# Which engine adds up the adaLN products for layer 3 while ConvFFN 2 runs

## The chip, the cores and the metric

One core of one Trainium2 chip runs the whole network as one program. The metric is the device time of one execution in microseconds; three executions of the kernel before took 1762.29, 1764.65 and 1765.87 us (median 1764.65). The tensor engine (PE) multiplies, the vector engine (DVE) and the scalar engine (ACT) work on tiles, GpSimd (POOL) works on tiles too and issues some transfers, and SyncE (SP) issues the weight transfers. Each engine executes its own queue strictly in order.

## The reference, cut to what matters

Four layers, each a token mixer followed by a gated convolutional feed-forward block (ConvFFN). Every sub-layer is modulated by six vectors per layer (adaLN) that come from one product of a condition vector with a large matrix:

```python
cond_lat = jax.nn.silu(c)
for i in range(DEPTH):
    mod_lat = (cond_lat @ ada_w[i] + ada_b[i])[:, None, :]      # 1024 x 6144 per layer
    sh1, sc1, g1, sh2, sc2, g2 = jnp.split(mod_lat, 6, axis=-1)
    ...
    h_lat = h_lat + g1 * y_lat
    v_lat = _modulate(_rmsnorm(h_lat, norm2_g[i]), sh2, sc2)
    h_lat = h_lat + g2 * _conv_ffn(v_lat, ...)

def _conv_ffn(u, w_up, conv_w, conv_b, w_down):
    hid = u @ w_up                                   # 1024 -> 5632
    hid = <depthwise convolution over 3 tokens>(hid) + conv_b
    val, gate = jnp.split(hid, 2, axis=-1)
    return (jax.nn.silu(gate) * val) @ w_down        # 2816 -> 1024
```

In layers 2 and 3 the blocks of interest work on the 256 latent tokens alone, and layer 3 needs its adaLN vectors for one condition only.

## The kernel before, in words

**ConvFFN.** `ffn` (L758) keeps PE supplied. Activations and weights are split into a high and a low part, and each product is three matmuls (`mm3`). The up-projection runs in 22 "pairs" f (one value tile, one gate tile, 48 matmuls of 256 columns), the down-projection in four parts of 8 output tiles d. Pairs and downs alternate: pairs 0 to 7, down of part 0, six pairs, down of part 1, and so on. Each pair writes two of four PSUM buffers `p`, so pair f+2 can start only when DVE has read pair f.

**What DVE does for each pair**, in the order of its queue for one condition: `al` (L819, low part of an earlier pair's activation, which the down-projection reads), a product `t` (L810), four convolution taps `t<-p` (L55; the last to read the pair's PSUM), and two subtractions `wlo` (L159) that make the low part of a weight block whose high part `whi` ACT has made. The end of `wlo` also frees the raw weight tile, so that SP can fetch the next block.

**The adaLN sums.** The product with `ada_w` is not done by PE directly. `ada_vec` (L297) is a generator with one step per loaded weight tile (`ada`, 1 MB, two buffers). It multiplies each tile by the condition values per partition and adds it to a running sum `ads`; at the end PE adds the sum over the partitions (`adp`) and turns it into columns (`adt`, `ada_turn`). `ffn` spreads the steps over its slots: `ada_slot` is called once after each pair and after every second d of the first three downs. Which engine adds is a letter per chunk: with "V" it is one operation on DVE, with "P" ACT multiplies in place and POOL adds:

```python
if i == 0:
    self.act(y, w[:, k], AF.Copy, scale=x)
elif eng == "V" or eng == "M" and i < 2:
    self.stt(y, w[:, k], x, y, ALU.mult, ALU.add)
else:
    ...
    self.act(t, w[:, k], AF.Copy, scale=x)
    self.nc.gpsimd.tensor_add(y, y, t)
```

The chunks of ConvFFN 2 are (layer 3, columns from 4, 4 wide), 8 tiles with one operation of 128x2048 each, and (layer 3, from 8, 2 wide), 4 tiles with two operations of 128x1024 each. In both, the first tile is written by ACT. Their tiles are fetched from POOL's queue (`ada_load`, L249), when the buffer before is free. The code puts a step behind the two `wlo` of its pair and ahead of the next pair's `al`.

Of the kernel before, what the change touches and what calls it, by code (L numbers as in the profile page):

```python
# [16 lines left out]
P = 128  # L17
# [27 lines left out]
class Net:  # L45
# [1929 lines left out]
    def run(self):  # L1975
        tc, nc, a = self.tc, self.nc, self.a
        with ExitStack() as es:
            pool = lambda n, **k: es.enter_context(tc.tile_pool(name=n, **k))
            self.cp = pool("cp", bufs=1)
            self.wp = pool("wp", bufs=1)  # L1980
            self.tp = pool("tp", bufs=1)
            self.up_ = pool("up_", bufs=1)
            PS = bass.MemoryType.PSUM
            self.psu = pool("psu", bufs=4, space=PS)
            self.psa = pool("psa", bufs=2, space=PS)
            self.psm = pool("psm", bufs=1, space=PS)
            es.enter_context(tc.manual_schedule())
            self.consts()
            blocks, glu0 = [], 0
            for l in range(DEPTH):  # L1990
                if l == 1:
                    glu0 = len(blocks)
                    blocks += [a["glu"][dp, kh] for dp, kh in GLU]
                if l == 2:
                    blocks += [a["qkv"][b] for b in (8, 9, 10, 11, 4, 0, 5, 1, 6, 2, 7, 3)] + [a["wo"][b] for b in range(4)]
                blocks += self.ffn_blocks(l)
            self.init_stream(blocks, 2, 2)
            self.limit = 0
            LC, LO = (0, 1), (0,)
            self.s5room = ExitStack()  # L2000
            self.sp = self.s5room.enter_context(tc.tile_pool(name="s5t", bufs=1, side="right"))
            with tc.tile_pool(name="s5p", bufs=1) as tp:
                self.start(tp, glu0)
            if self.stop == 4:
                return self.dump()

            tables = self.s5_tables()
            self.add_bg(tables)
            self.s5tab = {}
            self.ffn(0, LC, self.after_ffn(LC, self.s5_ahead), [(0, 10, 2), (1, 0, 4), (1, 4, 2)])  # L2010
            self.finish(tables)
            self.run_due(True)
            self.finish()
            if self.stop == 5:
                return self.dump()
            self.s5_mixer(1)
            self.finish()
            if self.stop == 10:
                return self.dump()
            self.ffn(1, LC, self.after_ffn(LC), [(1, 10, 2, "VV"), (2, 0, 4, "VV"), (2, 4, 4, "V"),  # L2020
                                                   (2, 8, 4, "P"), (3, 0, 4, "V")])
            self.finish()
            if self.stop == 11:
                return self.dump()
            self.nat_mixer(2)
            pm = self.pool_load(3)

            def pool_in(d):
                if d == 0:
                    self.pool_w(3, pm)  # L2030
                    self.pool_win(pm)
                    self.ada_init([(3, 10, 2, "M")], 1, (self.up_, self.u_bufs, 0, 2))
                    self.ada_ahead()

            self.ffn(2, LO, self.after_ffn(LO, pool_in), [(3, 4, 4, "P"), (3, 8, 2, "P")])
            r = self.rstd()
            us = self.pool_u(3, LO, r)
            self.sq_pe_start(LO)
            self._prep()
            self.pool_bias(3, 1, LO, pm)  # L2040
            for gp in range(2):
                self.pool_z(LO, pm, us, gp)
                next(self.ada_gen)
            self.pool_y(LO, pm, range(KD))
            self.ada_steps = [2, 6, 0, 0]
            self.r = self.rstd()
            self.ffn(3, LO, self.after_ffn(LO), None)
            self.final()
# [120 lines left out]
```

## Time and profile before

| what | value |
|---|---|
| median of three executions | 1764.65 us |
| the profiled execution | 1761.2 us, its span 1759.4 us |
| PE busy in the span | 1648.6 us (94%) |
| DVE busy | 1326.9 us (75%) |
| ACT busy | 804.5 us (46%) |
| POOL busy | 432.3 us (25%) |
| chain that ended last | PE 66%, DVE 13%, DMA 4%, ACT 4%, issue 4%, POOL 2% |

The span is what the trace covers; the execution's own time is 1.8 us longer. The busy shares are averages over all stages. ConvFFN 2 runs from about 1311 to 1532 us of the span, ConvFFN 3, of the same shape, from about 1560 to 1749 us. A timeline row gives start, duration, engine, line, operation, and in square brackets the idle time of the engine before it with what released it. A row of grouped instructions gives count, total busy time, mean duration in ns of one, and the idle time before them.

### The profile page before, as it was taken

How to read it: one execution, taken by the hardware profiler on the slowest of the kernel's cores; microseconds unless marked ns; L12 is line 12 of the kernel's file. 1: busy time of each engine (PE TensorE's matmuls, PEld its weight loads, DVE VectorE, ACT ScalarE, POOL GpSimd, SP SyncE). 2: the span in 40 equal slices, each digit the busy share in tenths (PEclk: the TensorE clock that was granted, in tenths of full speed). 3: DMA queues.
4: the chain of work that ended last, by engine and by line, in shares of the span. 5: the costliest groups of instructions: out<-in, count | busy, mean ns of one | idle time of the engine just before them, and what ended most of it. 6: DMA issues, size and time to landing. Idle time of an engine off the chain costs nothing.

```text
span 1759.4 us, 26668 instructions
## 1 busy us (share of the span) xinstructions
PE 1648.6 (94%) x10482; PEld 1364.8 (78%) x10482; DVE 1326.9 (75%) x1994; ACT 804.5 (46%) x1249; POOL 432.3 (25%) x330
## 2 busy tenths in 40 slices
PE   8889999998978899899999989999998799999998
PEld 4467777777768787687877867777688799889997
DVE  6768878899759667787877787546658889679776
ACT  4533323223253322643342634447657556475554
POOL 0015456574529301000000521102213404101001
PEclk9999999999998799999999999999999999999999
DMA  9658898787769644343548474333246666645553
GB/s 381 268 198 251 276 315 252 204 232 209 237 236 366 275 158 167 141 152 141 189 144 311 161 255 134 115 105 108 82 150 234 227 204 197 223 160 176 185 184 112
DMA packets 98182, 356.88 MB, mean 203 GB/s; under 512 B 14297, under 2 KB 37369, under 8 KB 72201
## 3 DMA queue, kind: packets, MB, share of 16 engines
q1 hardware_dynamic: 93400, 334.09, 56.2%
q0 software_dynamic: 4080, 18.99, 3.0%
q8 instruction: 83, 1.36, 0.3%
q10 hardware_dynamic: 576, 2.10, 0.3%
q14 instruction: 43, 0.34, 0.1%
HBM read 324.19 MB, written 30.94 MB: 202 GB/s over the span
## 4 chain that ended last, share of the span: by engine, by line
PE 66%; DVE 13%; DMA 4%; ACT 4%; issue 4%; POOL 2%; SPq 1%; DVEq 0%; ACTq 0%; POOLq 0%
PE p L61 33%; PE dn L61 15%; DVE wlo L159 5%; PE glu L61 4%; PE v L61 3%; PE k L61 2%; DVE t L55 2%; DMA s5fl<-s5dA 2%; PE wo L61 1%; PE q L61 1%; PE z L61 1%; PE adp L61 1%; ACT whi L58 1%; DVE al L819 1%; DMA raw<-in_wup_dram 1%
## 5 line engine op out<-in xcount | busy, mean ns | idle before, releaser
L61 PE MATMUL p<-uh,whi 128*128 128x512 f32 (+1 forms) x1408 | 485.5, 345 | 25.7 <-DVE t L55 15.3
L159 DVE TENSOR_TENSOR wlo<-raw,whi 128x1024 fp32r<-128x1024 f32 x334 | 401.2, 1243 | 123.3 <-ACT whi L58 122.1
L61 PE MATMUL p<-uh,wlo 128*128 128x512 f32 (+1 forms) x1408 | 480.0, 341 | 4.3 <-DVE wlo L159 2.5
L61 PE MATMUL p<-ul,whi 128*128 128x512 f32 (+1 forms) x1408 | 480.9, 342 | 0.1
L58 ACT ACTIVATE whi<-raw 128x1024 fp32r<-128x1024 f32 x352 | 318.3, 952 | 259.8 <-PE dn L61 83.4
L61 PEld LDWEIGHTS p<-uh,whi 128*128 128x128 f32 x1408 | 271.4, 193 | 68.9 <-issue 14.8
L61 PEld LDWEIGHTS p<-uh,wlo 128*128 128x128 f32 x1408 | 271.0, 192 | 35.8 <-DVE wlo L159 3.5
L61 PEld LDWEIGHTS p<-ul,whi 128*128 128x128 f32 x1408 | 271.3, 193 | 31.2 <-DVE ul L55 2.3
L61 PE MATMUL dn<-ah,wlo 128*128 128x512 f32 (+1 forms) x704 | 239.6, 340 | 8.5 <-DVE wlo L159 8.5
L61 PE MATMUL dn<-ah,whi 128*128 128x512 f32 (+1 forms) x704 | 240.9, 342 | 6.9 <-DVE h L55 4.1
L61 PE MATMUL dn<-al,whi 128*128 128x512 f32 (+1 forms) x704 | 239.0, 340 | 5.1 <-DVE al L819 5.1
L55 DVE SCALAR_TENSOR_TENSOR t<-p,conv_sb,t 128x510 f32<-128x510 f32 (+1 forms) x352 | 208.1, 612 | 27.3 <-ACT t L58 21.0
L321 POOL TENSOR_TENSOR ads<-ads,ada 128x2048 f32<-128x2048 f32 (+1 forms) x24 | 95.0, 3967 | 402.2 <-ACT ada L58 391.5
L61 PEld LDWEIGHTS dn<-ah,whi 128*128 128x128 f32 x704 | 134.9, 192 | 30.6 <-issue 10.2
L61 PEld LDWEIGHTS dn<-ah,wlo 128*128 128x128 f32 x704 | 134.8, 192 | 25.4 <-DVE wlo L159 10.9
L61 PEld LDWEIGHTS dn<-al,whi 128*128 128x128 f32 x704 | 134.6, 191 | 19.7 <-DVE al L819 5.6
L58 ACT ACTIVATE t<-p,conv_sb 128x512 f32<-128x512 f32 (+1 forms) x176 | 107.5, 660 | 49.5 <-PE p L61 49.4
L55 DVE SCALAR_TENSOR_TENSOR ads<-ada,cT_sb,ads 128x2048 f32<-128x2048 f32 (+1 forms) x56 | 116.7, 2116 | 8.1 <-DMA ada<-in_ada_dram 5.5
L55 DVE SCALAR_TENSOR_TENSOR h<-dn,mods,h 128x256 f32<-128x256 f32 x192 | 83.7, 476 | 40.8 <-PE dn L61 40.8
L58 ACT ACTIVATE ah<-t 128x512 fp32r<-128x512 f32 (+1 forms) x88 | 45.9, 523 | 148.9 <-DVE t L810 139.0
L58 ACT ACTIVATE t<-t 128x512 f32<-128x512 f32 (+1 forms) x88 | 45.9, 521 | 145.4 <-DVE t L55 137.7
L1316 POOL TENSOR_TENSOR s5ct<-s5bc,s5pw 128x512 f32<-128x512 f32 x32 | 44.1, 1377 | 219.5 <-DMA s5bc<-in_s5c_dram 144.5
(256 smaller groups left out, 2337.1 us busy)
## 6 DMA issues: line engine op xcount, KB each, us to landing
raw<-in_wup_dram SPq DMA_DIRECT2D x88, 1024.0 KB, 5.2
ada<-in_ada_dram SPq DMA_DIRECT2D x84, 1024.0 KB, 7.7
raw<-in_wdn_dram SPq DMA_DIRECT2D x32, 768.0 KB, 4.5
raw<-in_wdn_dram SPq DMA_DIRECT2D x32, 640.0 KB, 4.0
raw<-in_qkv_dram SPq DMA_DIRECT2D x12, 1024.0 KB, 5.0
ada<-in_ada_dram POOLq DMA_DIRECT2D x12, 1024.0 KB, 5.4
s5bt<-in_s5bT_dram SPq DMA_DIRECT2D x32, 256.0 KB, 7.4
s5fl<-s5dA SPq DMA_DIRECT2D x32, 256.0 KB, 7.1
```

The lines of the kernel that those rows point to most:

```text
L55: return self.nc.vector.scalar_tensor_tensor(out, in0, scalar, in1, op0=op0, op1=op1, **kw)
L58: return self.nc.scalar.activation(out, in_, func, **kw)
L61: return self.nc.tensor.matmul(out, lhsT, rhs, start=start, stop=stop)
L159: self.nc.vector.tensor_sub(lo[:, s], t[:, s], hi[:, s].bitcast(F32))
L321: self.nc.gpsimd.tensor_add(y, y, t)
L819: V.tensor_sub(lo[:, :n], tv, hi[:, :n].bitcast(F32))
L1316: G.tensor_tensor(ct[:, o], *x, op=ALU.mult)
```

## The change

In the chunks that ConvFFN 2 carries for layer 3, the letter "P" becomes "V":

```diff
-            self.ffn(2, LO, self.after_ffn(LO, pool_in), [(3, 4, 4, "P"), (3, 8, 2, "P")])
+            self.ffn(2, LO, self.after_ffn(LO, pool_in), [(3, 4, 4, "V"), (3, 8, 2, "V")])
```

So 7 + 6 multiplications on ACT and 7 + 6 additions on POOL are replaced by 7 + 6 `scalar_tensor_tensor` operations on DVE. The first tile of each chunk, the slots, the buffers and the queue of the `ada` transfers stay as they are.

DVE's queue around pairs 2 and 3 of ConvFFN 2, before (`p_...` are the PSUM tiles of a pair, `ads_4_0` the running sum of the first chunk, `ada_4_n` its tile n):

```order
L159 TENSOR_TENSOR wlo_10820<-raw_10681,whi_10817 128x1024 x2
L819 TENSOR_TENSOR al_10880<-t,ah_10879 128x256
L810 TENSOR_TENSOR t<-t 128x256
L55 SCALAR_TENSOR_TENSOR t<-p_10758,conv_sb,t 128x255 x2
L55 SCALAR_TENSOR_TENSOR t<-p_10759,conv_sb,t 128x255 x2
L159 TENSOR_TENSOR wlo_10895<-raw_10756,whi_10892 128x1024 x2
L819 TENSOR_TENSOR al_10955<-t,ah_10954 128x256
```

The same place on DVE now:

```order
L159 TENSOR_TENSOR wlo_10820<-raw_10681,whi_10817 128x1024 x2
L55 SCALAR_TENSOR_TENSOR ads_4_0_10685<-ada_4_1_10530,cT_sb,ads_4_0_10685 128x2048
L819 TENSOR_TENSOR al_10879<-t,ah_10878 128x256
L810 TENSOR_TENSOR t<-t 128x256
L55 SCALAR_TENSOR_TENSOR t<-p_10758,conv_sb,t 128x255 x2
L55 SCALAR_TENSOR_TENSOR t<-p_10759,conv_sb,t 128x255 x2
L159 TENSOR_TENSOR wlo_10894<-raw_10756,whi_10891 128x1024 x2
L55 SCALAR_TENSOR_TENSOR ads_4_0_10685<-ada_4_2_10687,cT_sb,ads_4_0_10685 128x2048
L819 TENSOR_TENSOR al_10953<-t,ah_10952 128x256
```

A sum stands ahead of `al` and of the taps that free the pair's PSUM; nothing else has moved.

POOL's queue for the first chunk, before:

```order
L255 DMA ada_4_2_10687<-in_ada_dram 128x2048
L321 TENSOR_TENSOR ads_4_0_10685<-ads_4_0_10685,ada_4_1_10530 128x2048
L255 DMA ada_4_3_10827<-in_ada_dram 128x2048
L321 TENSOR_TENSOR ads_4_0_10685<-ads_4_0_10685,ada_4_2_10687 128x2048
L255 DMA ada_4_4_10902<-in_ada_dram 128x2048
```

POOL's queue at the same place now:

```order
L255 DMA ada_4_2_10687<-in_ada_dram 128x2048
L255 DMA ada_4_3_10826<-in_ada_dram 128x2048
L255 DMA ada_4_4_10900<-in_ada_dram 128x2048
L255 DMA ada_4_5_11045<-in_ada_dram 128x2048
L255 DMA ada_4_6_11132<-in_ada_dram 128x2048
```

The additions are gone; a transfer into a buffer now waits for the sum on DVE that reads it last, where it stood behind the addition on POOL.

## Rows read from the trace of the kernel before

**Rows 1.** Busy time per stretch: all ConvFFN 3, all ConvFFN 2, three parts of it.
```profile
core 0: us, PE busy (x) PEld busy (x) DVE busy (x) ACT busy (x) POOL busy (x), PEclk, DMA share, GB/s
1559.70:1749.00 189.30, 188.50 (x1602) 186.81 (x1604) 154.20 (x254) 112.19 (x183) 15.59 (x10) 0.99 0.51 168
1311.40:1531.60 220.20, 203.45 (x1618) 198.54 (x1620) 184.06 (x257) 132.69 (x196) 59.93 (x29) 0.95 0.64 221
...
1341.40:1411.40 70.00, 56.72 (x417) 55.09 (x417) 60.98 (x65) 40.17 (x52) 33.58 (x14) 0.89 0.63 219
...
1471.40:1491.40 20.00, 16.77 (x136) 16.05 (x135) 19.79 (x25) 11.10 (x19) 6.82 (x3) 1.00 0.44 143
...
1411.40:1451.40 40.00, 40.00 (x334) 39.03 (x333) 33.22 (x58) 22.40 (x37) 0.00 (x0) 0.98 0.63 211
```

**Rows 2.** Timeline of PE: matmuls with idle time before them.
```profile
1344.78 0.36 PE L61 MATMUL p<-uh,whi 128*128 128x256 f32 x1 [1.92 <-ACT ah L58]
...
1353.08 0.36 PE L61 MATMUL p<-uh,whi 128*128 128x256 f32 x1 [1.81 <-DVE t L55]
...
1373.47 0.58 PE L61 MATMUL dn<-al,whi 128*128 128x256 f32 x1 [4.86 <-DVE al L819]
...
1406.76 0.55 PE L61 MATMUL p<-uh,whi 128*128 128x256 f32 x1 [3.42 <-DVE t L55]
```

**Rows 3.** Timeline of DVE, first chunk.
```profile
1338.54 4.85 DVE L819 TENSOR_TENSOR al<-t,ah 128x256 fp32r<-128x256 f32 x1
...
1366.49 1.90 DVE L55 SCALAR_TENSOR_TENSOR t<-p,conv_sb,t 128x255 f32<-128x255 f32 x4
1368.31 4.77 DVE L159 TENSOR_TENSOR wlo<-raw,whi 128x1024 fp32r<-128x1024 f32 x2
...
1383.81 10.06 DVE L159 TENSOR_TENSOR wlo<-raw,whi 128x1024 fp32r<-128x1024 f32 x2 [0.77 <-ACT whi L58]
```

**Rows 4.** Timeline of POOL, first chunk.
```profile
1337.43 5.67 POOL L321 TENSOR_TENSOR ads<-ads,ada 128x2048 f32<-128x2048 f32 x1 [7.37 <-ACT ada L58]
...
1366.82 4.57 POOL L321 TENSOR_TENSOR ads<-ads,ada 128x2048 f32<-128x2048 f32 x1
...
1382.60 4.62 POOL L321 TENSOR_TENSOR ads<-ads,ada 128x2048 f32<-128x2048 f32 x1 [10.36 <-ACT ada L58]
...
1388.09 4.69 POOL L321 TENSOR_TENSOR ads<-ads,ada 128x2048 f32<-128x2048 f32 x1
```

**Rows 5.** Instructions by line and shape, DVE, 1320 to 1520 us.
```profile
L159 DVE TENSOR_TENSOR wlo<-raw,whi 128x1024 fp32r<-128x1024 f32 x54 | 87.8, 1657 | 17.1 <-ACT whi L58 16.9
...
L819 DVE TENSOR_TENSOR al<-t,ah 128x256 fp32r<-128x256 f32 x22 | 20.1, 912 | 3.3 <-ACT ah L58 3.1
```

**Rows 6.** Instructions by line and shape, DVE, 1620 to 1740 us.
```profile
L159 DVE TENSOR_TENSOR wlo<-raw,whi 128x1024 fp32r<-128x1024 f32 x38 | 45.2, 1220 | 12.1 <-ACT whi L58 12.0
...
L819 DVE TENSOR_TENSOR al<-t,ah 128x256 fp32r<-128x256 f32 x14 | 5.9, 419 | 0.1
```

**Rows 7.** The sums on DVE in ConvFFN 1, 600 to 970 us, by shape.
```profile
L55 DVE SCALAR_TENSOR_TENSOR ads<-ada,cT_sb,ads 128x2048 f32<-128x2048 f32 x35 | 83.1, 2404 | 0.9 <-DMA ada<-in_ada_dram 0.5 <-ACT ads L58 0.3
L55 DVE SCALAR_TENSOR_TENSOR ads<-ada,cT_sb,ads 128x1024 f32<-128x1024 f32 x12 | 14.7, 1277 | 0.0
```

**Rows 8.** Timeline of DVE: two successive `al` with one undisturbed pair between.
```profile
1473.37 0.41 DVE L819 TENSOR_TENSOR al<-t,ah 128x256 fp32r<-128x256 f32 x1
...
1478.12 0.42 DVE L819 TENSOR_TENSOR al<-t,ah 128x256 fp32r<-128x256 f32 x1
```

**Rows 9.** Chain that ended last: matmuls behind the wait at 1406.76 (start, us, what).
```profile
1406.76 14.41 PE p L61 x96
```

**Rows 10.** Transfers of the `ada` tiles, 1300 to 1500 us, from issue.
```profile
DMA to landing us min/median/max: 5.1/5.4/9.4
```

**Rows 11.** Instructions by line and shape, ACT, 1320 to 1520 us.
```profile
L58 ACT ACTIVATE ada<-ada,cT_sb 128x2048 f32<-128x2048 f32 x7 | 14.0, 1994 | 0.0
```

## Prediction, made before the result was known

> **What bounds the kernel now.** I read the page first: PE is busy 94% of the span, so only the stretches where PE waits can give time back. Then I set the two ConvFFNs of the same shape side by side, busy time per stretch. ConvFFN 3 takes 189.3 us, ConvFFN 2 220.2 us for nearly the same matmuls (1602 and 1618 recorded) [rows 1]. Of these 30.9 us, two stretches of ConvFFN 2 carry most: from 1341.4 to 1411.4 PE starts 417 matmuls in 70 us, from 1471.4 to 1491.4 136 in 20 us, while between the two it starts 334 in 40 us, 8.35 a microsecond [rows 1]. At that pace 417 need 49.9 us and 136 need 16.3 us: 20.1 + 3.7 = 23.8 us are lost there. They are the stretches in which POOL adds (33.58 and 6.82 us busy) and DVE is nearly full.
>
> Next the timeline of PE: it waits 1.92, 1.81, 4.86 and 3.42 us for the taps or for `al` [rows 2], all DVE's work or next to it. The timeline of DVE then shows why DVE is late. An `al` that takes 0.42 us elsewhere takes 4.85 us, the two `wlo` of a block 4.77 and 10.06 us [rows 3], and each of these lies across one or two of POOL's additions: the `al` of 1338.54 ends at 1343.39, the addition at 1343.10; the 10.06 us cover the additions of 1382.60 and 1388.09 [rows 3, 4]. The four taps that start at 1366.49 while POOL adds from 1366.82 take their usual 1.90 us [rows 3, 4]. So DVE's two-tile operations from SBUF stand still while POOL adds, and the taps, which take one tile from PSUM, do not.
>
> The Trainium skill says the same ("SBUF — State Buffer", Who interferes with whom): a DVE instruction with two SBUF inputs contends with a GpSimd instruction that reads SBUF, and the later one blocks until the other is done. The trace agrees, with the rows just named. It has a rule against this change too ("Perfetto Trace Analysis", Optimizing Scalar/DVE Operations): where DVE is saturated, handing work to Scalar or even GpSimd may make sense. By that rule putting 24 us on DVE costs time, and it is weighed below as the rival that ends slower.
>
> **What goes.** The 13 additions on POOL, and with them the stretched rows. Between 1320 and 1520 us `wlo` averages 1657 ns over 54, `al` 912 ns over 22 [rows 5]; in ConvFFN 3 past POOL's last addition of that kind they average 1220 and 419 ns [rows 6]. 54 x 0.437 + 22 x 0.493 = 23.6 + 10.8 = 34.4 us of DVE's time are standstill. The 13 multiplications on ACT go as well, 14.0 us for the seven large ones [rows 11], but ACT is busy 132.69 of 220.2 us [rows 1] and I price that at nothing.
>
> **What comes.** 7 operations of 128x2048 and 6 of 128x1024 on DVE. In ConvFFN 1 the same operations take 2404 and 1277 ns [rows 7]: 16.8 + 7.7 = 24.5 us. These too have two SBUF inputs, but POOL has nothing beside them now but transfer issues. DVE's load falls by 34.4 - 24.5 = 9.9 us. That is the lower bound of the gain if DVE alone set the pace of both stretches; the upper bound is the 23.8 us that PE loses there.
>
> **Between the bounds: pair by pair.** An undisturbed pair takes DVE 1478.12 - 1473.37 = 4.75 us from `al` to `al` [rows 8], PE 48 / 8.35 = 5.75 us. A pair with a sum takes DVE 4.75 + 2.4 = 7.15 us, so sums on successive pairs make DVE late by 1.4 us each, and pairs without one give 1.0 back. Of the pair's 4.75 us I give 0.7 to `al` and the product, 1.8 to the taps, 2.25 to the `wlo`, 1.5 where the block is one of the smaller down-projection blocks. From 1338.5, where the first sum now stands:
> - sum 1 to 1340.9, pair 3 with its taps from 1341.6 to 1345.7 at its end; sum 2 to 1348.1, pair 4 (taps from 1348.8) to 1352.8; pair 5 without a sum (taps from 1353.5) to 1357.1; sum 3 to 1359.5, pair 6 to 1363.7; sum 4 to 1366.1, then the `al` of pair 5, done at 1366.5.
> - PE stands at the end of pair 4 at 1344.78 - 1.92 = 1342.9. Pair 5 needs half of pair 3's taps, ready at 1342.5: no wait. It ends at 1348.6; pair 6 waits for pair 4's taps to about 1349.8, with a second short wait 1.4 us in all. Pair 7 runs without a wait to 1361.6. The down of part 0 does 15 matmuls (1.8 us) and then waits for that `al`, from 1363.4 to 1366.5: 3.1 us. Its other 129 take 15.4 us, to 1381.9; two pairs more end at 1393.4. DVE has sums 5 to 7 in this down (7.2 us), four weight blocks (some 8 us) and eight short additions into h, less than the 26.9 us that PE needs from 1366.5 to 1393.4, so the taps for the next pair are not late.
> - Before, this pair started at 1406.76 [rows 2]. The gain is 13.3 us.
>
> Two smaller terms. After the wait that ends at 1406.76, 96 matmuls take 14.41 us [rows 9] where 8.35 a microsecond makes 11.5: 2.9 us at a lowered clock (the granted clock is 0.89 on average in the first stretch against 0.98 behind it [rows 1]). That goes, and I let the new 3.1 us wait cost the same 2.9 us: nothing. In the second stretch three steps of 2 x 1.28 us fall on four pairs: 4 x 4.75 + 3 x 2.55 = 26.7 us of DVE against 23.0 of PE; PE is ahead of DVE by little there, but DVE enters the stretch with idle time, so I take 3.2 of the 3.7 us. **Sum: 13.3 + 3.2 = 16.5 us.**
>
> What could take the sums' cover away is their data. A sum waits at the head of DVE's queue for its `ada` tile, and behind it stand `al`, the taps and `wlo`, for which PE waits. A tile's transfer starts when the sum two before it is done, and successive odd (or even) sums lie 11 to 18 us apart in the list above, while a transfer takes 5.4 us, at most 9.4 [rows 10]. Hidden; a tile that took 15 us would put some 4 us on PE. Where the sum is waited for, at the end of a chunk (`adp`), there are five slots of lag: nothing. SP's queue keeps its order; `wlo` ending sooner only starts weight transfers sooner.
>
> The profiled execution took 1761.2 us, span and 1.8 us beside it, 3.45 us below the median of the three runs. It becomes 1761.2 - 16.5 = 1744.7; against the median 1764.65 - 16.5 = 1748.1 us, and I forecast 1748.
>
> **Rivals.**
> 1. DVE alone paces the stretches (the sums also pull `wlo`, and with it weights, behind): 9.9 us, 1754.7. For it: two successive sums delay DVE by 2.8 us in a stretch where PE has no lead. Against it: pairs without a sum give time back, and DVE idles between the chunks. 0.2.
> 2. All that PE loses comes back, since PE's PSUM buffers and lead cover sums: 23.8 us, 1740.8. For it: ConvFFN 3 runs at full pace with DVE busy 154.20 of 189.3 us [rows 1], and ConvFFN 2 would have 184.06 - 9.9 = 174 in about 200. Against it: my replay, two waits of 1.4 and 3.1 us. 0.17.
> 3. Slower: the long rows on DVE are not POOL's doing but come from something that stays, say the tile transfers that run in the same stretches. Then the change adds 24.5 us to a queue that has 70 - 60.98 = 9.0 us idle in the first stretch and 0.2 in the second [rows 1]: 16.8 - 9.0 + 7.7 - 0.2 = 15.3 us, 1780. That is the offloading rule's result. It decides as soon as less than 24.5 of the 34.4 us go, and then only past DVE's idle time. Against it: between 1411.4 and 1451.4 the transfers run as hard (211 against 219 GB/s [rows 1]) with POOL idle, and PE loses nothing. 0.05.
> 4. Nothing to see: the standstill goes, and as much is waited for elsewhere (weights, a late `ada` tile): within 3.5 us of 1764.65. 0.03.
>
> **How the numbers follow.** The forecast has the rest, 0.55. Measurement tells about 0.2%, 3.5 us, from no change. Faster: forecast, rivals 1 and 2, 0.92; same 0.03; slower 0.05. The range reaches from below rival 2 (1740.8, less the 2 us that runs differ by) to past rival 1 (1754.7, plus 3): 1739 to 1758, and leaves out rivals 3 and 4 and the edges.
>
> **What would show it.** Right: no POOL additions between 1320 and 1500; `wlo` and `al` there at about 1.22 and 0.42 us; the 13 sums at 2.4 and 1.28 us without a wait for DMA; PE waiting for an `al` in the first down by about 3 us and little else; ConvFFN 2 about 204 us, ConvFFN 3 unchanged. Wrong: `wlo` still at 1.6 us, sums that wait for `ada`, or new waits of PE for `wlo`.

## The result and the profile after

The changed kernel takes 1741.74 us (median of four, 1740.51 to 1745.49) against 1763.47 us for the kernel before on the same chips: ratio 0.9881, 95% interval 0.9864 to 0.9897. A second set of runs gave 0.9896 (0.9881 to 0.9910). The forecast was 1748 in a range of 1739 to 1758: direction and range held, the gain is 21.7 us where 16.5 were forecast.

The profiled execution after took 1745.49 us, the longest of its four; it enters ConvFFN 2 4.6 us later than the trace of before (1316.01 against 1311.43), in stages that the change does not touch. So the stage itself is compared, not the span. The busy time per stretch after (columns as in rows 1): all ConvFFN 2, the 70 us that answer to before's first stretch, 10 us inside it, and all ConvFFN 3.

```profile
1316.00:1515.10 199.10, 195.49 (x1620) 192.33 (x1620) 170.68 (x271) 114.26 (x183) 10.32 (x16) 0.98 0.71 245
1345.90:1415.90 70.00, 66.75 (x550) 65.14 (x548) 64.75 (x91) 36.46 (x60) 3.54 (x6) 0.98 0.78 266
1371.20:1381.20 10.00, 10.00 (x77) 10.00 (x76) 9.58 (x15) 4.35 (x6) 0.13 (x1) 0.84 0.81 290
1543.70:1733.00 189.30, 188.40 (x1602) 186.85 (x1601) 153.23 (x252) 111.17 (x182) 15.65 (x10) 0.99 0.51 168
```

ConvFFN 2 is down from 220.2 to 199.1 us, ConvFFN 3 is the same 189.3 us [rows 1]. In the first stretch PE starts 550 matmuls in 70 us where it started 417 [rows 1].

The groups of DVE by line and shape, after, 1320 to 1515 us:

```profile
L159 DVE TENSOR_TENSOR wlo<-raw,whi 128x1024 fp32r<-128x1024 f32 x56 | 66.6, 1219 | 12.6 <-ACT whi L58 12.4
...
L55 DVE SCALAR_TENSOR_TENSOR ads<-ada,cT_sb,ads 128x2048 f32<-128x2048 f32 x7 | 16.4, 2346 | 0.0
...
L819 DVE TENSOR_TENSOR al<-t,ah 128x256 fp32r<-128x256 f32 x22 | 9.2, 420 | 4.1 <-ACT ah L58 4.0
...
L55 DVE SCALAR_TENSOR_TENSOR ads<-ada,cT_sb,ads 128x1024 f32<-128x1024 f32 x6 | 7.4, 1278 | 0.0
```

`wlo` and `al` stand at 1219 and 420 ns where they averaged 1657 and 912 [rows 5], as in the undisturbed stretch of before [rows 6]. The 13 sums take 16.4 + 7.4 = 23.8 us, and the 0.0 behind them says that none waited for its tile, though the longest of their transfers took 9.9 us to land.

The timeline of DVE around the fourth sum, and the matmuls of PE with idle time before them in the first stretch (they answer to rows 3 and rows 2); the last row is the first matmul of pair 10, which starts without a wait:

```profile
1366.96 2.35 DVE L55 SCALAR_TENSOR_TENSOR ads<-ada,cT_sb,ads 128x2048 f32<-128x2048 f32 x1
1369.22 0.42 DVE L819 TENSOR_TENSOR al<-t,ah 128x256 fp32r<-128x256 f32 x1
```

```profile
1353.30 0.35 PE L61 MATMUL p<-uh,whi 128*128 128x256 f32 x1 [0.54 <-DVE t L55]
...
1354.20 0.36 PE L61 MATMUL p<-uh,whi 128*128 128x256 f32 x1 [0.32 <-DVE t L55]
...
1369.70 0.39 PE L61 MATMUL dn<-al,whi 128*128 128x256 f32 x1 [2.39 <-DVE al L819]
...
1397.53 0.28 PE L61 MATMUL p<-uh,whi 128*128 128x256 f32 x1
```

PE waits twice for taps behind two successive sums, and once for the `al` that stands behind the fourth sum: the two places of the forecast, a little smaller. Past them the chain that ended last stays on PE through both stretches (start, us, what; 48 matmuls of `p` are a pair):

```profile
1386.39 22.66 PE p L61 x192
...
1439.31 45.37 PE p L61 x384
```

### The profile page after: what moved, and what is told of

The parts are those of the page before. It is cut to its first block, busy times and chain, and to the rows that moved or that the text cites. A ratio compares the mean times of both kernels' runs of the same rounds, so it can differ in the third digit from the quotient of the medians.

```text
span 1743.7 us, 26649 instructions
## 1 busy us (share of the span) xinstructions
PE 1642.7 (94%) x10482; PEld 1359.1 (78%) x10482; DVE 1317.5 (76%) x2007; ACT 785.2 (45%) x1236; POOL 382.2 (22%) x317
## 4 chain that ended last, share of the span: by engine, by line
PE 59%; DVE 17%; DMA 5%; issue 4%; ACT 4%; POOL 3%; SPq 1%; DVEq 0%; ACTq 0%; POOLq 0%
PE p L61 28%; PE dn L61 14%; DVE wlo L159 5%; PE glu L61 4%; DMA s5fl<-s5dA 4%; DVE t L55 3%; PE v L61 2%; PE k L61 2%; PE wo L61 1%; ACT whi L58 1%; PE q L61 1%; DVE s5bt L1328 1%; DVE s5vt L1327 1%; DVE h L55 1%; PE z L61 1%
## 5 line engine op out<-in xcount | busy, mean ns | idle before, releaser
L159 DVE TENSOR_TENSOR wlo<-raw,whi 128x1024 fp32r<-128x1024 f32 x334 | 378.2, 1174 | 118.6 <-ACT whi L58 117.4
L55 DVE SCALAR_TENSOR_TENSOR t<-p,conv_sb,t 128x510 f32<-128x510 f32 (+1 forms) x352 | 208.2, 612 | 25.6 <-ACT t L58 19.3
L55 DVE SCALAR_TENSOR_TENSOR ads<-ada,cT_sb,ads 128x2048 f32<-128x2048 f32 (+1 forms) x69 | 140.5, 2066 | 6.6 <-DMA ada<-in_ada_dram 5.0
L321 POOL TENSOR_TENSOR ads<-ads,ada 128x2048 f32<-128x2048 f32 (+1 forms) x11 | 45.6, 4157 | 345.1 <-ACT ada L58 334.5
```

Source lines behind the costliest of these rows:

```text
L55: return self.nc.vector.scalar_tensor_tensor(out, in0, scalar, in1, op0=op0, op1=op1, **kw)
L159: self.nc.vector.tensor_sub(lo[:, s], t[:, s], hi[:, s].bitcast(F32))
```

## The experiments

Times of whole executions differ by several us between runs (the changed kernel's four by 5.0 us, the seven of the kernel before on one chip by 12.6). The length of ConvFFN 2 in the traces differs less. So for each kernel stand the median and its ratio to the kernel before on its chip, and the us from the stage's first matmul to its end (the sum of squares `ssq`), split at the first matmuls of the two `adp` that close the chunks: up to the first covers the first stretch, between the two the second stretch, and behind it nothing changes. The changed kernel was traced twice. The first 48 matmuls of the stage lie ahead of every sum and addition, and yet take from 7.7 us (changed) to 8.7 (second chunk only), 8.6 in before's trace: over the first 10 us the granted clock is 0.83 in the changed kernel's trace and 0.71 in before's. So differences of 1 us between two rows can be chance.

| kernel | median, ratio (95%) | stage | to first `adp` | between | behind |
|---|---|---|---|---|---|
| before | 1763.47 (first set) | 221.3 | 109.7 | 80.1 | 31.5 |
| changed | 1741.74, 0.9881 (0.9864 to 0.9897) | 200.1 | 93.0 | 75.6 | 31.5 |
| changed, second trace | 1742.57, 0.9896 (0.9881 to 0.9910) | 200.4 | 93.0 | 75.8 | 31.5 |
| first chunk only | 1746.17, 0.9912 (0.9889 to 0.9935) | 205.0 | 93.4 | 80.1 | 31.5 |
| second chunk only | 1756.36, 0.9966 (0.9949 to 0.9983) | 215.2 | 108.0 | 75.6 | 31.5 |
| POOL adds beside | 1764.37, 1.0016 (1.0002 to 1.0029) | 222.0 | 107.4 | 83.1 | 31.5 |
| short sums | 1737.41, 0.9860 (0.9835 to 0.9885) | 195.0 | 87.9 | 75.6 | 31.5 |
| POOL memsets beside | 1742.60, 0.9888 (0.9855 to 0.9921) | 201.0 | 93.6 | 75.8 | 31.5 |
| ACT multiplies beside | 1742.23, 0.9884 (0.9850 to 0.9918) | 200.4 | 93.0 | 75.8 | 31.5 |
| spread steps | 1739.65, 0.9867 (0.9830 to 0.9904) | 197.1 | (moved) | | |
| all sums on DVE | 1733.65, 0.9829 (0.9786 to 0.9872) | 201.1 | 93.7 | | |
| all on DVE, spread | 1727.65, 0.9813 (0.9800 to 0.9827) | 196.5 | (moved) | | |

Medians of different rows come from different chips; the ratios compare.

**Each chunk alone.**

```diff
-            self.ffn(2, LO, self.after_ffn(LO, pool_in), [(3, 4, 4, "V"), (3, 8, 2, "V")])
+            self.ffn(2, LO, self.after_ffn(LO, pool_in), [(3, 4, 4, "V"), (3, 8, 2, "P")])
```

and for the second, the letters the other way round.

> Only the first chunk's sums (7 operations of 128x2048) go to DVE; the second chunk's stay with ACT and POOL. Theory A (POOL's additions stop DVE's operations with two SBUF inputs, each stretch loses by itself): the first stretch's part of the gain, some 17 to 18 of the 21.7 us, so 1745 to 1747 us, and the waits of PE around the second chunk stay as before (about 3 us). Rival B (what is gained is the load of ACT and of POOL's queue as a whole, shared by both chunks in proportion to the operations' time): about two thirds of 21.7, so 1749 us.

> Only the second chunk's sums (6 operations of 128x1024) go to DVE; the first chunk's stay with ACT and POOL. Theory A: only the second stretch's loss comes back, 3 to 4 us, so about 1760 us, with PE's waits of 1.8 to 4.9 us in the first stretch as before. Rival B: a third of the gain, about 1756 us. If the two parts add up to the whole, the stretches are independent.

The first chunk gives 109.7 - 93.4 = 16.3 us and leaves the second stretch at 80.1; the second gives 80.1 - 75.6 = 4.5 us there. Each stretch moves with its own chunk, which is what theory A says and what a load shared by both would not do. The sizes decide less. Of the 16.3 us, some 0.9 lie in the first 48 matmuls, and the rest stands between A's 17 or 18 and two thirds of the stage's 21.2, which are 14.1. The execution times do not tell A from B: against the kernel before on their chip (1761.92 us) the two gain 15.8 and 5.6 us, and both theories lie in the intervals of the ratios. In the trace of the second chunk alone the first stretch is 1.7 us shorter than in before's, with POOL's additions there: most of it is in pairs 10 and 11, which take 13.15 us for 14.41 [rows 9], at a granted clock of 0.88 over the first 13 us where before has 0.77. What lets the clock rise sooner in one trace is not shown.

**POOL's additions beside the sums.**

```diff
                             self.stt(y, w[:, k], x, y, ALU.mult, ALU.add)
+                            if l == 3 and b0 in (4, 8):
+                                e = self.ap_.tile([P, 1024], F32, tag="extra", name="extra", bufs=1)
+                                for o in range(0, n, 1024):
+                                    v = w[:, k, o:o + 1024]
+                                    self.nc.gpsimd.tensor_add(e, v, v)
...
+        self.ap_ = ap_
```

> The changed kernel, and beside each sum on DVE POOL adds the same tile to itself into a scratch tile, in pieces of 128x1024, whose result nobody reads; ACT has nothing more to do. Theory A: wlo, al and now the sums too are stretched wherever they meet an addition; DVE carries 24.5 us of sums and the standstill, and the time is above that of the kernel before: 1765 to 1790 us. Rival (POOL's additions are not what stretched DVE's rows): wlo and al stay at 1.22 and 0.42 us and the time stays at 1742, plus or minus 3 us.

The stage rises from 200.1 to 222.0 us and the whole gain is gone: the rival, 1742, is refuted. The size just misses A's range (1764.37 for 1765 to 1790); it is 2.5 us above the kernel before on this chip. Groups by line and shape, this kernel, 1320 to 1510 us:

```profile
L159 DVE TENSOR_TENSOR wlo<-raw,whi 128x1024 fp32r<-128x1024 f32 x51 | 77.9, 1558 | 8.0 <-ACT whi L58 7.9
L159 DVE TENSOR_TENSOR wlo<-raw,whi 128x512 fp32r<-128x512 f32 x8 | 8.9, 1106 | 0.0
L320 POOL TENSOR_TENSOR extra<-ada 128x1024 f32<-128x1024 f32 x20 | 49.6, 2479 | 1.1
L55 DVE SCALAR_TENSOR_TENSOR ads<-ada,cT_sb,ads 128x2048 f32<-128x2048 f32 x7 | 17.2, 2463 | 0.0
L55 DVE SCALAR_TENSOR_TENSOR ads<-ada,cT_sb,ads 128x1024 f32<-128x1024 f32 x6 | 10.7, 1821 | 0.0
```

POOL adds for 49.6 us, and DVE stands still for 51 x (1.558 - 1.219) = 17.3 us in the large `wlo`, 3.4 us in those of 128x512 (8.9 for 5.5 in the changed kernel) and 0.8 + 3.3 us in the sums: 24.8 us, not 34.4. The stage grew by 21.9. No `al` meets an addition here. Each two additions stand in POOL's queue behind the issue of a tile's transfer, which waits for its buffer, and in six of ten cases the first of the two starts beside the taps, as in these rows of POOL's timeline and DVE's:

```profile
1345.75 4.75 POOL L320 TENSOR_TENSOR extra<-ada 128x1024 f32<-128x1024 f32 x2
```

```profile
1345.21 1.90 DVE L55 SCALAR_TENSOR_TENSOR t<-p,conv_sb,t 128x255 f32<-128x255 f32 x4
1347.02 4.55 DVE L159 TENSOR_TENSOR wlo<-raw,whi 128x1024 fp32r<-128x1024 f32 x2
```

The taps keep their 1.90 us while POOL adds, the `wlo` behind them take 4.55 for 2.35. What POOL costs depends on which of DVE's operations it meets. That this makes the whole difference between 24.8 and 34.4 us is not shown: these additions are also shorter, and read one tile where before they read two.

**POOL writes, but reads nothing.** In place of the additions `self.nc.gpsimd.memset(e, 0.0)`, as often.

> The changed kernel, and beside each sum POOL writes zeros into a scratch tile of 128x1024 (two per tile of 2048 columns), reading nothing. It tells whether POOL's reading or any work of POOL on SBUF stops DVE. Theory A in the form with reads: wlo and al stay within a few per cent of 1.22 and 0.42 us, time 1742 plus or minus 3 us. Rival (any POOL operation on SBUF does it): wlo and al are stretched as in the kernel before and the time rises by 10 us or more.

Groups by line and shape, this kernel, 1320 to 1510 us:

```profile
L159 DVE TENSOR_TENSOR wlo<-raw,whi 128x1024 fp32r<-128x1024 f32 x56 | 66.6, 1219 | 13.1 <-ACT whi L58 13.0
...
L320 POOL MEMSET extra<- 128x1024 f32 x20 | 19.3, 963 | 0.6
```

POOL is busy 19.3 us on the same scratch tile and DVE does not notice. That is not for want of meeting it: 13 of the large `wlo` run beside a memset, for 8.3 us together, and none takes more than 1.23 us (no `al` met one). Timeline of POOL and of DVE:

```profile
1449.52 4.02 POOL L320 MEMSET extra<- 128x1024 f32 x4
```

```profile
1450.59 2.35 DVE L159 TENSOR_TENSOR wlo<-raw,whi 128x1024 fp32r<-128x1024 f32 x2
```

So an operation of POOL that only writes SBUF does not stop DVE, and one that also reads it does. This is the Trainium skill's rule in the form that it has ("SBUF — State Buffer", Who interferes with whom): contention with a GpSimd instruction that reads SBUF, not with one that only writes it.

**ACT multiplies as before.** In place of the additions `self.act(e, v, AF.Copy, scale=x)`.

> The changed kernel, and beside each sum ACT multiplies the tile by the condition value into a scratch tile, in pieces of 128x1024, as much as ACT did before for these chunks; nobody reads the result. Theory A: ACT has room, 1742 to 1744 us. Rival (part of the gain was ACT's freed time, whi or ah coming earlier): 5 us or more of the 21.7 are lost again, 1747 us and up.

200.4 against 200.1 and 200.4 us: ACT's freed time carries nothing of the gain.

**Sums cut short.**

```diff
-                            self.stt(y, w[:, k], x, y, ALU.mult, ALU.add)
+                            m = 16 if l == 3 and b0 in (4, 8) else n
+                            self.stt(y[:, :m], w[:, k, :m], x, y[:, :m], ALU.mult, ALU.add)
```

> The changed kernel with each of the 13 sums in ConvFFN 2 cut to its first 16 columns, so the layer 3 vectors of these chunks are not computed in full; waits and transfers stay. It prices the sums on DVE. Theory A with the trace after: PE still waits 0.5, 0.3 and 2.4 us and loses about 1 us to the clock because of the sums, so 4 us less: 1737 to 1738 us. Rival C (DVE still sets the pace of the stage, each microsecond of sums costs one): up to 24 us less, 1718 us. Rival D (the sums are hidden in full): no change, 1742 us.

The stage is 195.0 us. Of the 23.8 us of sums on DVE, PE notices 200.1 - 195.0 = 5.1 (5.4 by the second trace), all in the first stretch (93.0 to 87.9). The rest is hidden beside matmuls. DVE does not set the pace of the stage any more; cutting the sums would have given back up to 24 us otherwise. The first 48 matmuls take 8.4 us here, so the sums may cost some 0.7 us more than 5.1.

**Steps further apart.**

```diff
-            self.ada_init(adas, NF + (12 if l else 0), l and ((ap_, 4, 0, 2) if full else (self.up_, self.u_bufs, 5, 4)))
+            self.ada_init(adas, NF + (12 if l else 0), l and ((ap_, 4, 0, 2) if full else (self.up_, self.u_bufs, 3, 4)))
```

> The changed kernel with 3 instead of 5 idle steps behind each chunk, so that the steps lie further apart: of the first chunk's sums three instead of four stand before the first down. Theory A (what is left of PE's waits comes from the fourth sum ahead of the al that the first down needs): the 2.4 us wait goes and the clock loss of about 1 us with it: 1738 to 1739 us. Rival (the waits move to pairs 8 to 13, where the sums now lie, or the end of the second chunk comes too late): 1741 us or more.

The stage is 3.0 us shorter than the changed kernel's (3.3 by its second trace); the execution time alone, with its interval, would not tell that from nothing. PE's wait for the `al` of the first down, 2.39 us in the changed kernel, is down to 1.0, not gone: the third sum now stands ahead of that down. Behind it the granted clock stays at 1.00.

**The other chunks of POOL too.**

```diff
-                                                   (2, 8, 4, "P"), (3, 0, 4, "V")])
+                                                   (2, 8, 4, "V"), (3, 0, 4, "V")])
...
-                    self.ada_init([(3, 10, 2, "M")], 1, (self.up_, self.u_bufs, 0, 2))
+                    self.ada_init([(3, 10, 2, "V")], 1, (self.up_, self.u_bufs, 0, 2))
```

The first line belongs to ConvFFN 1, the second to ConvFFN 3.

> The changed kernel with the two other chunks that POOL adds moved to DVE too: 7 operations of 128x2048 in ConvFFN 1, and 4 of 128x1024 in ConvFFN 3. Theory A: in ConvFFN 1 PE waits 4.7 us for wlo and 1.5 for whi beside POOL's additions and runs at a lowered clock after it, some 6 to 9 us in all; in ConvFFN 3 it waits 0.8 us. Time 1732 to 1737 us. Rival (DVE in ConvFFN 1, which works on 512 columns, has no room for 16.5 us more): no gain, 1742 us or more.

1733.65 us, as theory A has it. Busy time per stretch in ConvFFN 1, where POOL's seven additions were, first the changed kernel, then this one:

```profile
980.00:1060.00 80.00, 73.85 (x321) 58.88 (x320) 64.50 (x65) 37.63 (x41) 34.27 (x7) 0.96 0.63 225
```

```profile
980.00:1060.00 80.00, 79.77 (x360) 64.52 (x359) 69.17 (x80) 29.40 (x39) 0.00 (x0) 1.00 0.72 252
```

PE starts 39 matmuls more in the same 80 us; at 4.5 a microsecond that is 8.7 us.

**Both together.**

> The two edits that each gained are put together: every chunk that POOL adds goes to DVE, and ConvFFN 2 has 3 idle steps behind a chunk. If the stages are independent, as the two chunks were: the 8 us of the first edit and the 3 us that ConvFFN 2 became shorter by the second add up, 1730 us plus or minus 3, ratio to the kernel before 0.981. Rival (the later end of the second chunk, or sums of ConvFFN 3 on DVE, take it back): 1734 us or more.

> The changed kernel itself, beside the previous one on the same chip, so that both ratios have the same runs of the kernel before: 1741 to 1743 us, ratio 0.988; the difference to the combined kernel 11 us by theory A.

1727.65 us, ratio 0.9813 (0.9800 to 0.9827), beside 1742.57 us and 0.9896 for the changed kernel on the same chip: 33.7 us faster than the kernel before and 14.9 us faster than the changed one. This is the fastest version of the study. The time lies in the expected 1730 plus or minus 3; the difference of 14.9 is more than the 11 expected, and why is not shown.

## Why the prediction was right, and where its size was off

- **The standstill goes.** Right. `wlo` and `al` are back at 1219 and 420 ns; additions on POOL that nobody needs bring back 24.8 us of standstill and 21.9 us of stage, and memsets bring back none.
- **The sums cost 24.5 us on DVE.** They take 23.8.
- **Replay of the first stretch, 13.3 us up to pair 10.** Before, that pair starts 1406.76 - 1311.43 = 95.3 us into the stage; after, two pairs of the four in the 22.66 us lie before it, and it starts 1397.53 - 1316.01 = 81.5 us in (the row is shown with the result). That is 13.8 us sooner, but 0.9 of it lies in the stage's first 48 matmuls, where nothing had changed. This part is luck; without it the gain is 12.9. In the second trace of the changed kernel, whose first matmuls are as slow as before's, it is 14.1. The waits were 0.9 us for taps (1.4 forecast) and 2.39 us for `al` (3.1 forecast).
- **The clock term, priced at nothing.** This is the term that was mis-sized. I took the 2.9 us that the lowered clock cost behind the wait of 3.42 us before pair 10 [rows 9], and let the new wait cost them again. The first half held: from the start of pair 10 to the first `adp` it is 14.4 us before and 11.5 after, 2.9 less. The second half did not. In the 10 us from 1371.2, behind the new wait, the granted clock is 0.84 and PE starts 77 matmuls, where it starts 87 in an undisturbed slice, so about 1.1 us, and that lies ahead of pair 10, inside the 13.8. In the second trace of the changed kernel the same wait of 2.39 us cost no clock at all (1.00, 87 matmuls). So 2.9 us were missing from the sum.
- **Second stretch, 3.2 us.** It gave 4.5: PE waits for no taps there any more. I had kept back 0.5 of the 3.7, and the pace of 8.35 matmuls a microsecond by which I counted the loss was low: undisturbed, 384 take 45.37 us, which is 8.46.
- **Sum.** 13.8 + 2.9 + 4.5 = 21.2 us, and the stage is 221.3 - 200.1 = 21.2 us shorter. The forecast's 16.5 lacked the 2.9 of the clock, 1.3 of the second stretch and 0.5 up to pair 10, which the luck of the first matmuls more than covers.
- **Rivals.** DVE as the pace of the stretches (9.9 us) is refuted by the short sums: 5.1 of 23.8 us reach PE. Full recovery (23.8 us, 1740.8) was the nearest in size, nearer to the measured 1741.74 than the forecast's 1748. It was not full: the sums still cost 5.1 us, and the bound was too low, since with the sums cut short the stage is 221.3 - 195.0 = 26.3 us shorter than before. "Slower" and "nothing to see" are out.
- **The offloading rule** of the Trainium skill ("Perfetto Trace Analysis", Optimizing Scalar/DVE Operations) would have kept the additions on GpSimd, DVE being the fuller engine. Here 33.3 + 16.1 = 49.4 us of additions on POOL cost DVE 34.4 us, the same sums on DVE 23.8. Its own next sentence, that the two share an SBUF read port so that moving work between them might not help, is the part that the measurement bears out.

## What to carry to other kernels

An engine that looks free is not free if its reads stop another: look for one operation with two very different durations in the trace, lay its long rows beside the other engine's timeline, and count the excess as the price of the offload. Whether the work then fits on the loaded engine is a matter of where it stands in the queue: go through the queue operation by operation around the place where a wait ends last. A wait of PE can cost again afterwards, by the granted clock, and a change that removes waits gets that back too; the same wait does not cost it in every execution.

## What the runs showed of the hardware that was not expected

- DVE's operations with two inputs in SBUF were stretched whatever their kind: `wlo` (1219 to 1558 ns), and the sums themselves (1278 to 1821 ns), which are `scalar_tensor_tensor`; the taps of that same kind, with one input in PSUM, kept 479 ns.
- 49.4 us of additions on POOL came with 34.4 us of standstill of `al` and `wlo` in the kernel before, and 49.6 us of other, shorter additions at other moments with 24.8.
- POOL waits as well: in the kernel with the additions beside, the piece that starts at 1345.75 beside the taps takes 1.91 us, the next, from 1347.73 beside `wlo`, 2.77.
- The granted clock behind one and the same wait differs from trace to trace. Behind the `al` wait of 2.39 to 2.41 us it averages 0.84 over 10 us in two traces (changed, first chunk only) and 1.00 in four (changed again, memsets, ACT multiplies, all sums on DVE). 1.00 is the upper of the clock's two levels (2.4 GHz); 0.84 is an average over a stretch that lay at the lower one (1.2 GHz) for a part of its time. The 10 us from 1.5 us past the end of that wait, in the second trace of the changed kernel, where the first has 77 matmuls at 0.84:

```profile
1366.90:1376.90 10.00, 10.00 (x87) 10.00 (x87) 9.71 (x15) 4.35 (x6) 0.35 (x1) 1.00 0.83 291
```
